# Mixer A of a two-block network on one core: two heads stacked on the rows, directions as planes of one tile, level products over 64 rows

## The chip, the core and the metric

The kernel runs on one core of one Trainium2 chip. The metric is the device time of one execution in microseconds (us), from the first to the last instruction and what the runtime adds around them. A core has five instruction streams: TensorE (PE, whose weight loads are shown apart as PEld), VectorE (DVE), ScalarE (ACT), GpSimd (POOL) and SyncE (SP, which here only issues DMAs). Each stream runs in its own order and waits on semaphores of the others.

## The reference

The network has two layers of a first block and then one second block, on 512 latent tokens and 256 context tokens of width 1024, all in float32. A layer of the first block projects the tokens, runs four mixers A to D on 256 features each, gates their outputs, projects them back and normalises. Only mixer A is touched by the change. It is a gated linear recurrence with four heads of 64 features, run forwards and backwards, with forget gates f of their own for either direction:

```python
def gla_chunk_scan(q, k, v, logf, s0):
    """S_t = diag(f_t) S_{t-1} + k_t^T v_t ; o_t = q_t S_t"""
...
o_f, _ = gla_chunk_scan(q, k_f, i, lf_f, s_cf)
o_b, _ = gla_chunk_scan(flip(q), flip(k_b), flip(i), flip(lf_b), s_cb)
y = merge_heads(rms_norm(o_f + flip(o_b), norm_g))
```

Here k = 1 - f for each direction, q is silu of a projection, and i is the value. The latent scans start from the final state of the context (in layer 0 the context's outputs are wanted too, so 768 queries; in layer 1 only the 512 latent ones).

## The kernel before

Tokens are cut into chunks of 128 (six of them, four latent and two of the context). Within a chunk the products q_t k_s times the gates between s and t are found by doubling: `level_mm` is called once for the diagonal and once for each of seven levels i, with h = 2^i. At level i a block of 2h tokens meets: in the forward direction the queries of the upper half see the keys of the lower half, in the backward direction the queries of the lower half see the keys of the upper one. A mask `m8` picks from the 128 x 128 products those that belong to the level (`copy_predicated` into `att`). After the products of a level, q and k are multiplied by the gates of half a block (`T` holds these gates, multiplied together pair by pair), ready for the next level.

Before the change the 128 rows (partitions) of a tile hold one head: rows 0 to 63 its forward direction, rows 64 to 127 its backward one. `co_head` does one head, and `j_a` spawns it for both heads of a pair, so that two such generators go on side by side; pairs follow one another. At each level `co_head` makes `Qm`, a copy of `Qh` in which the queries that the level doesn't want are zeroed (mask `mq`); the matmul of a chunk then contracts over all 128 rows, both directions at once:

```python
self.mul("*", Qm.rearrange("p (c t) -> p c t", t=128), Qh.rearrange("p (c t) -> p c t", t=128), mq)
...
nc.tensor.matmul(ps[:, cc], Kh[:, cc], Qm[:, cc], start=True, stop=True)
```

Then four multiplications of 64 rows each bring `Qh` and `Kh` to the next level, and one brings `T` there. Two DMAs for each head copy the queries `qs` into the two halves of `Qm`. At the end of a head the keys are transposed, their products with the values `va` give the state's increments (`up`), and a chain of multiply-adds gives the state `Si` before each chunk. When both heads are done, `j_a` multiplies `att` by the values and `Si` by `Qh`, into a bank that `headnorm` reads.

The order of the work is not written by hand. The program keeps generators in flight (attention units, mixer A, normalisations) and a list of fillers (the projections, whose weights come by DMA and are split into two fp32r parts `whi` and `wlo`); while instructions are emitted, class `Est` estimates when each engine and each piece of data will be ready, and `turn` emits what could start first on PE, a filler if nothing else can. `best` chooses between DVE, POOL and ACT for an operation marked "*" by the same estimates. Each engine then runs its own stream in that order. A filler's products are three matmuls of fp32r; mixer A's are plain float32, which the trace shows as two records for each matmul. Every operation goes through one helper, so all rows of the profile carry the line L283; the names tell them apart. `banks` is PSUM, `kh`, `qh`, `qm`, `att`, `si`, `T`, `f` are the tiles named above (`si` is the state), `p` the probabilities of the attention mixers, `h` the projected tokens.

Of the kernel before, what the change touches and what calls it, by code (L numbers as in the profile page):

```python
# [13 lines left out]
AF = mybir.ActivationFunctionType  # L14
# [10 lines left out]
# column starts in w_in of the first block  # L25
# [25 lines left out]
# broadcast rows  # L51
# [37 lines left out]
def pack(inp):  # L89
# [40 lines left out]
    put("lb", g["hg_lb_logits"].reshape(2, 2, 4, 64).transpose(1, 3, 0, 2))  # L130
# [26 lines left out]
    # constants of the shapes  # L157
# [6 lines left out]
    mq = [np.where(p < 64, (t >> i) & 1, 1 - ((t >> i) & 1)) for i in range(7)]  # L164
    ms = [((p >> (i + 1)) == (t >> (i + 1))) & ((p >> i) != (t >> i)) for i in range(7)]
    a["masks"] = np.stack(mq + ms, axis=1).astype(f)
# [5 lines left out]
    # second block  # L172
# [32 lines left out]
class Quiet:  # L205
    """Stands for an engine while lifetimes are recorded."""
# [5 lines left out]
class Est:  # L212
    """Estimates, while instructions are emitted, of when engines and data will be ready: the order of emission follows."""
# [7 lines left out]
    def touch(self, ap):  # L221
        """The times of a tensor and the granules of it (128 elements) that ap covers."""
# [44 lines left out]
class Eng:  # L267
    """An engine whose instructions are timed as they are emitted."""
# [37 lines left out]
class Act:  # L306
    """Work in flight: a generator that yields what it waits for."""
# [6 lines left out]
class Tl:  # L314
    """A piece of SBUF with its own tensor."""
# [14 lines left out]
class Mem:  # L330
    """SBUF by lifetimes. A first emission (plan None) only records them; place() then gives each piece its address."""
# [82 lines left out]
class Pb:  # L414
    """Banks of PSUM."""
# [9 lines left out]
class Psum:  # L425
# [3 lines left out]
    def pick(self, n, est):  # L429
        """The free banks that have been read first, and when."""  # L430
# [28 lines left out]
class K:  # L459
# [18 lines left out]
    # ---- short forms  # L478
# [48 lines left out]
    def scale(self, out, a, s):  # L527
        """out = a times a column s."""
# [21 lines left out]
    # ---- time  # L550
    def time(self, eng, op, outs, ins, kw):
# [11 lines left out]
        if eng == "P":  # L563
            if op == "transpose":
                c = 107.0
            else:
# [27 lines left out]
    # ---- work in flight  # L594
# [11 lines left out]
    def after(self, *keys):  # L606
        """Until no work of these keys is in flight."""
# [70 lines left out]
    def choose(self):  # L678
        """Takes up the first filler for which there is room."""
# [37 lines left out]
    # ---- weights  # L717
# [28 lines left out]
    def more(self):  # L746
        """Weights of a further filler."""
# [17 lines left out]
    def g_fm(self, parts, evac):  # L765
        """parts: [(hi, lo, n)]; evac(i, bank) for each."""
# [1749 lines left out]
```

## Time and profile before

| | |
|---|---|
| median of 3 runs | 2021.99 us (2017.59, 2021.99, 2022.09) |
| span of the profiled execution | 2020.4 us, 1.6 us below the median; its time with what lies around the span is not given apart |
| instructions | 28590 |
| mixer A, layer 0 | about 191 to 476 us: the first pair of heads to 325 us, the second from 359 us |
| mixer A, layer 1 | about 814 to 1016 us |
| second block | from about 1150 us to the end, not touched |

Busy times are unions of the records of a group; the length of a matmul record includes its way through the array, so consecutive ones overlap, and what one costs is read from start to start. An idle engine costs nothing unless the end waits for it; here the stream to watch is PE's.

### The profile page before, as it was taken

Reading aid. Unit: us, or ns where it says so; the run is one execution under the profiler, and the core shown is the slowest. Engines: PE = TensorE matmul, PEld = TensorE weight load, DVE = VectorE, ACT = ScalarE, POOL = GpSimd, SP = SyncE. Lnnn points to the kernel's source line nnn. Section 1 sums busy time; section 2 is a strip of 40 time slices with the busy share of each in tenths; the row PEclk is TensorE's granted clock in tenths of the full one; section 3 lists DMA queues with packets and bytes.
Section 4 is the critical chain, followed back from the end, with each engine's and each line's share of the span. In section 5 each row is a group of like instructions: output and inputs, shape, how many; then the busy total and the mean of one; then the engine's idle time right before and its main releaser. Section 6 shows DMA issues by size and latency. Waiting matters only on the chain.

```text
span 2020.4 us, 28590 instructions
## 1 busy us (share of the span) xinstructions
PE 1892.4 (94%) x11270; PEld 1571.6 (78%) x11270; DVE 1295.5 (64%) x2202; ACT 621.0 (31%) x1274; POOL 636.4 (31%) x583
## 2 busy tenths in 40 slices
PE   6899889889999999979899989899999999999999
PEld 4688657789877788867787777877878787888887
DVE  2558885686557738787967878874533566545542
ACT  2245434414540135544335231143432211100100
POOL 1314662374232414565633353421121220000000
PEclk9999999999999999999999998999999999999999
DMA  8112241001132401103124221111232222233122
GB/s 348 53 32 71 72 142 47 17 17 57 32 115 84 157 1 43 38 21 106 43 63 141 98 101 66 67 58 48 81 128 87 99 73 84 83 115 115 53 84 73
DMA packets 46807, 162.32 MB, mean 80 GB/s; under 512 B 5312, under 2 KB 5824, under 8 KB 46416
## 3 DMA queue, kind: packets, MB, share of 16 engines
q1 hardware_dynamic: 43648, 151.63, 21.9%
q10 hardware_dynamic: 3024, 8.85, 1.3%
q8 instruction: 89, 1.46, 0.3%
q14 instruction: 46, 0.38, 0.1%
HBM read 152.58 MB, written 5.26 MB: 78 GB/s over the span
## 4 chain that ended last, share of the span: by engine, by line
PE 41%; DVE 11%; POOL 3%; issue 2%; ACT 2%; DMA 0%; ACTq 0%; DVEq 0%; POOLq 0%
PE banks L283 41%; DVE cacc L283 2%; POOL t L283 1%; DVE sm L283 1%; DVE wlo L283 1%; DVE kh L283 1%; DVE t L283 1%; ACT p L283 1%; DVE att L283 1%; DVE p L283 1%; DVE h L283 1%; DVE whi L283 0%; POOL h L283 0%; DMA ld<-gws 0%; DVE gt L283 0%
## 5 line engine op out<-in xcount | busy, mean ns | idle before, releaser
L283 PE MATMUL banks<-h,whi 128*128 128x512 f32 (+1 forms) x1968 | 583.9, 380 | 4.4 <-ACT h L283 2.1
L283 PEld LDWEIGHTS banks<-h,whi 128*128 128x128 f32 x1968 | 353.6, 191 | 66.5 <-POOL h L283 2.5
L283 PE MATMUL banks<-h,wlo 128*128 128x512 f32 (+1 forms) x984 | 369.4, 376 | 0.3 <-DVE wlo L283 0.3
L283 PE MATMUL banks<-whi,h 128*128 128x256 f32 (+3 forms) x1344 | 336.1, 333 | 17.2 <-DVE h L283 7.9
L283 DVE TENSOR_TENSOR wlo<-raw,whi 128x1024 fp32r<-128x1024 f32 (+1 forms) x174 | 216.6, 1248 | 94.9 <-PE banks L283 59.5
L283 PEld LDWEIGHTS banks<-whi,h 128*128 128x128 f32 x1344 | 235.5, 193 | 41.9 <-DVE h L283 9.8
L283 POOL TENSOR_TENSOR wlo<-raw,whi 128x1024 fp32r<-128x1024 f32 (+2 forms) x42 | 103.4, 2464 | 482.8 <-PE banks L283 314.6
L283 PE MATMUL banks<-wlo,h 128*128 128x256 f32 (+3 forms) x672 | 220.2, 328 | 7.4 <-POOL wlo L283 3.7
L283 PEld LDWEIGHTS banks<-h,wlo 128*128 128x128 f32 x984 | 187.6, 191 | 35.8 <-DVE wlo L283 1.0
L283 ACT ACTIVATE p<-banks,sm 128x768 f32<-128x768 f32 (+5 forms) x192 | 141.3, 739 | 107.5 <-DVE sm L283 90.6
L283 DVE TENSOR_REDUCE sm<-banks 128x1 f32<-128x768 f32 (+5 forms) x192 | 139.9, 750 | 49.1 <-PE banks L283 41.4
L283 PE MATMUL banks<-whi,hid 128*128 128x512 f32 x512 | 159.5, 392 | 0.0
L283 DVE CAST whi<-raw 128x1024 fp32r<-128x1024 f32 (+2 forms) x105 | 79.3, 759 | 112.8 <-DMA raw<-wm 66.0
L283 PEld LDWEIGHTS banks<-wlo,h 128*128 128x128 f32 x672 | 129.7, 193 | 19.0 <-DVE wlo L283 5.0
L283 ACT CAST whi<-raw 128x1024 fp32r<-128x1024 f32 (+2 forms) x83 | 82.8, 1002 | 193.3 <-PE banks L283 98.1
L283 PEld LDWEIGHTS banks<-whi,hid 128*128 128x128 f32 x512 | 96.1, 188 | 21.5
L283 PE MATMUL banks<-ident,p 128*128 128x128 f32 x656 | 97.1, 278 | 15.7 <-ACT p L283 5.7
L283 ACT COPY p<-banks 128x768 f32<-128x768 f32 (+5 forms) x122 | 75.6, 626 | 106.5 <-PE banks L283 96.8
L283 PE MATMUL banks<-qm,kh 128*128 128x128 f32 x640 | 91.9, 294 | 17.3 <-DVE att L283 8.1
L283 PEld LDWEIGHTS banks<-qm,kh 128*128 128x128 f32 x640 | 83.1, 204 | 29.4 <-issue 9.8
L283 PEld LDWEIGHTS banks<-ident,p 128*128 128x128 f32 x656 | 74.5, 141 | 34.3 <-ACT p L283 8.7
L283 POOL TENSOR_TENSOR t<-t,mhalf 128x1 f32<-128x1 f32 (+5 forms) x51 | 64.4, 1266 | 115.9 <-DVE t L283 112.3
(331 smaller groups left out, 3220.8 us busy)
## 6 DMA issues: line engine op xcount, KB each, us to landing
raw<-wm SPq DMA_DIRECT2D x64, 512.0 KB, 3.7
raw<-win SPq DMA_DIRECT2D x60, 512.0 KB, 3.6
raw<-wada SPq DMA_DIRECT2D x48, 512.0 KB, 4.8
raw<-wgate SPq DMA_DIRECT2D x32, 512.0 KB, 3.2
raw<-wout SPq DMA_DIRECT2D x24, 512.0 KB, 3.5
raw<-w2f SPq DMA_DIRECT2D x10, 512.0 KB, 3.2
xr<-xtok SPq DMA_DIRECT2D x6, 512.0 KB
x<-z SPq DMA_DIRECT2D x6, 512.0 KB, 2.6
```

The costliest lines, as they stand in the source:

```text
L283: return f(*a, **kw)
```

## The change

Everything that mixer A does between the projections and its head norm is laid out anew. Rows 0 to 63 hold head 0 of the pair and rows 64 to 127 head 1; the two directions are planes of one tile ([128, 2, 768]). The units of `w_in` and the columns of the lower bounds are packed to fit. `j_a` does a whole pair in one generator (`co_head` is gone). At a level it copies the keys that the level wants, forward ones for lower halves and backward ones for upper halves, into `ks`; the wanted queries are read in place by a view that steps between the planes (`aview`). A chunk's products are then two matmuls of 64 rows, one for each head in turn, into two banks. `Qm`, its mask `mq`, the load of `mq` and the 16 DMAs of the queries are gone. The multiplications to the next level are one for q and one for k, over 128 rows. The products with the values have 64 instead of 128 stationary columns, the state is brought on by half as many instructions of 128 rows, and the last products add two of 64 rows for each head and chunk where one of 128 rows stood. The outputs are copied out in pieces of 64 rows, and the squares are taken from the copy. The estimate takes half the time for a matmul of 64 rows.

```diff
-        for h in range(4):
-            u.append(_fm_unit(np.concatenate([w[:, C_FF + 64 * h:C_FF + 64 * h + 64], w[:, C_FB + 64 * h:C_FB + 64 * h + 64]], 1)))
+        for j in range(2):
+            u += [_fm_unit(w[:, c + 128 * j:c + 128 * j + 128]) for c in (C_FF, C_FB)]
...
+                    if k.shape[0] == 64:
+                        c /= 2
...
-    def level_mm(self, Kh, Qm, att, i):
+    def aview(self, z, flip, h, o, n):
+        N = z.f.shape[2]
+        p, at = z.f.ap[0], z.f.offset + o + (N if flip else 0)
+        return bass.AP(z.f.tensor, at, [list(p), [2 * h, n // (2 * h)], [h - N if flip else N + h, 2], [1, h]])
...
+    def aparts(self):
+        return ((0, 4), (4, 2))[:1 + self.full]
...
+    def half(self, v, j):
+        return bass.AP(v.tensor, v.offset + 64 * j * v.ap[0][0], [[v.ap[0][0], 64]] + [list(x) for x in v.ap[1:]])
...
+    def level_mm(self, lhs, rhs, att, i, c0, n):
...
-        for c in range(nch):
-            cc = slice(c * 128, (c + 1) * 128)
-            nc.tensor.matmul(ps[:, cc], Kh[:, cc], Qm[:, cc], start=True, stop=True)
-        n = nch * 128
+        ps = self.new_bank(2)
+        for c in range(n):
+            k, q = lhs(c0 + c), rhs(c0 + c)
+            for j in range(2):
+                nc.tensor.matmul(ps[:, j * 512 + c * 128:j * 512 + (c + 1) * 128], self.half(k, j), self.half(q, j), start=True, stop=True)
...
         for i in range(7):
-            yield (Qh,)
-            mq = self.mq[:, i, :].unsqueeze(1).to_broadcast([128, nch, 128])
-            self.mul("*", Qm.rearrange("p (c t) -> p c t", t=128), Qh.rearrange("p (c t) -> p c t", t=128), mq)
-            yield (Qm, Kh, self.bank(nb))
-            self.level_mm(Kh, Qm, att, i)
             h = 1 << i
...
+            yield (KZ,)
+            ks = M.new([128, nq], tag="ks")
+            self.cp("*", ks.rearrange("p (b w h) -> p b w h", w=2, h=h), self.aview(KZ, False, h, 0, nq))
+            for c0, n in self.aparts():
+                yield (QZ, ks, self.bank(2))
+                self.level_mm(at(ks), lambda c: self.aview(QZ, True, h, c * 128, 128), att, i, c0, n)
...
-            for r0, up in ((0, 1), (64, 0)):
-                r = slice(r0, r0 + 64)
-                tq = Tv[r, :nbq, 1 - up].unsqueeze(2).to_broadcast([64, nbq, h])
-                tk = Tv[r, :, up].unsqueeze(2).to_broadcast([64, nbk, h])
-                self.mul("*", Qv[r, :, up], Qv[r, :, up], tq)
-                self.mul("*", Kv[r, :, 1 - up], Kv[r, :, 1 - up], tk)
...
+            for z, flip, n in ((QZ, True, nq), (KZ, False, NT)):
+                v = self.aview(z, flip, h, 0, n)
+                self.mul("*", v, v, self.tview(Tc, flip, o, n // (2 * h), h))
...
+                for j in range(2):
+                    hh, r = 2 * pair + j, slice(64 * j, 64 * j + 64)
+                    cc = slice(c * 128, (c + 1) * 128)
+                    out = ps[r, j * 512 + (c - c0) * 128:j * 512 + (c - c0 + 1) * 128]
+                    nc.tensor.matmul(out, self.va[:, c, hh * 64:hh * 64 + 64], att[:, j, cc], start=True, stop=False)
+                    for d in range(2):
+                        nc.tensor.matmul(out, S[r, d, c], QZ[r, d, cc], start=False, stop=d == 1)
```

PE's stream in layer 0, second pair, early levels, before the change (out<-moving,stationary; numbers are buffers; `qm_3158` and `qm_3166` belong to the two heads, the other rows are attention scores, transposes and a projection):

```order
L283 MATMUL banks<-qm_3158,kh_3161 128x128 x6
L283 MATMUL banks<-ident_70,stg_3322 128x128 x2
L283 MATMUL banks<-whi_2976,h_98 128x256
L283 MATMUL banks<-wlo_2977,h_98 128x256
L283 MATMUL banks<-whi_2976,h_99 128x256
...
L283 MATMUL banks<-qm_3166,kh_3169 128x128 x6
L283 MATMUL banks<-whi_2976,h_99 128x256
L283 MATMUL banks<-whi_2976,h_98 128x256
L283 MATMUL banks<-wlo_2977,h_98 128x256
L283 MATMUL banks<-whi_2976,h_99 128x256
L283 MATMUL banks<-qm_3158,kh_3161 128x128 x5
```

The same place after the change (`ks_2963` and `ks_3078` are the key copies of two successive levels; `p` rows are outputs of mixer B):

```order
L282 MATMUL banks<-qh_2840,ks_2963 128x128 x12
L282 MATMUL banks<-p_2871,bdv_720 64x128
L282 MATMUL banks<-p_2880,bdv_720 64x128
...
L282 MATMUL banks<-whi_3054,h_98 128x256
L282 MATMUL banks<-whi_3054,h_97 128x256
L282 MATMUL banks<-wlo_3055,h_97 128x256
L282 MATMUL banks<-whi_3054,h_98 128x256
L282 MATMUL banks<-qh_2840,ks_3078 128x128 x12
```

Two groups of six for a level, one for each head and some work apart, have become one group of twelve; between these two levels stand 44 other matmuls.

POOL's stream in the same place, before (`qm` rows make the masked queries, `qh` and `kh` rows bring queries and keys to the next level; x2 are two equal rows):

```order
L283 TENSOR_TENSOR qh_3162<-qh_3162,T_3164 64x192x2
L283 TENSOR_TENSOR kh_3161<-kh_3161,T_3164 64x192x2 x2
L283 TENSOR_TENSOR qh_3162<-qh_3162,T_3164 64x96x4
L283 TENSOR_TENSOR kh_3169<-kh_3169,f_2961 64x384
L283 TENSOR_TENSOR qm_3166<-qh_3170,mq_67 128x768
L283 TENSOR_TENSOR qh_3170<-qh_3170,T_3172 64x192x2 x2
```

And after:

```order
L282 TENSOR_TENSOR qh_2840<-qh_2840,T_2841 128x192x2x2
L282 TENSOR_TENSOR wlo_3055<-raw_2967,whi_3054 128x1024
L282 TENSOR_TENSOR kh_2839<-kh_2839,T_2841 128x96x2x4
L282 TENSOR_SCALAR p_3044<-p_3044,sm_3043 128x256
L282 TENSOR_TENSOR qh_2840<-qh_2840,T_2841 128x96x2x4
```

The masked copies are gone, and one multiplication of 128 rows stands for four of 64. Over the whole program all 28 multiplications of q to a next level stand on POOL afterwards, 23 of the 28 of k on DVE; DVE has 2055 instead of 2204 instructions, POOL 458 instead of 588, PE 10002 instead of 9914.

PE's stream at the last products of the second pair of layer 0, before (`att` and `si` rows of the two heads):

```order
L283 MATMUL banks<-att_3163,va_531 64x128
L283 MATMUL banks<-qh_3162,si_3773 64x128
L283 MATMUL banks<-att_3171,va_531 64x128
L283 MATMUL banks<-att_3163,va_531 64x128
L283 MATMUL banks<-qh_3162,si_3773 64x128
L283 MATMUL banks<-att_3171,va_531 64x128
L283 MATMUL banks<-qh_3170,si_3890 64x128
```

And after:

```order
L282 MATMUL banks<-att_2842,va_529 64x128
L282 MATMUL banks<-qh_2840,si_3446 64x128 x2
L282 MATMUL banks<-att_2842,va_529 64x128
L282 MATMUL banks<-qh_2840,si_3446 64x128 x2
L282 MATMUL banks<-att_2842,va_529 64x128
```

Three matmuls a head and chunk instead of two, the last two of them over 64 rows. Counted over the whole stream, the part of the array that a matmul uses (its rows and columns) changes from one matmul to the next 264 times before and 379 times after.

## Rows read from the trace of the kernel before

**Rows 1.** The page, busy us (share of the span) and instructions

```profile
PE 1892.4 (94%) x11270; PEld 1571.6 (78%) x11270; DVE 1295.5 (64%) x2202; ACT 621.0 (31%) x1274; POOL 636.4 (31%) x583
```

**Rows 2.** Busy time by stage: stage; length, PE, PEld, DVE, ACT, POOL; clock, DMA

```profile
100.00:191.00 91.00, 86.90 (x650) 77.47 (x649) 62.27 (x120) 43.41 (x96) 25.44 (x21) 1.00 0.08 24
191.00:320.00 129.00, 115.72 (x799) 82.33 (x799) 103.82 (x178) 57.17 (x124) 79.88 (x75) 0.99 0.36 117
320.00:450.00 130.00, 116.16 (x918) 104.16 (x919) 93.77 (x152) 47.70 (x98) 57.81 (x56) 0.93 0.07 19
450.00:600.00 150.00, 146.39 (x1128) 130.02 (x1127) 88.20 (x217) 68.40 (x167) 54.79 (x50) 1.00 0.21 68
...
800.00:920.00 120.00, 102.30 (x720) 88.81 (x718) 99.47 (x145) 52.09 (x94) 70.34 (x77) 0.96 0.11 34
920.00:1020.00 100.00, 94.66 (x781) 78.67 (x781) 82.11 (x144) 42.69 (x78) 60.49 (x70) 0.98 0.23 72
1020.00:1150.00 130.00, 126.60 (x788) 103.72 (x789) 94.96 (x172) 48.42 (x105) 42.26 (x35) 1.00 0.28 93
```

**Rows 3.** Waits of PE over the whole span: us, times, longest

```profile
PE banks L283 <- DVE att L283: 11.8, 9, 3.1
...
PE banks L283 <- POOL qm L283: 4.1, 2, 2.9
```

**Rows 4.** PE by form: records | busy us, mean ns | idle before

```profile
L283 PE MATMUL banks<-qm,kh 128*128 128x128 f32 x640 | 91.9, 294 | 17.3 <-DVE att L283 8.1 <-POOL qm L283 4.1 <-DVE qm L283 2.0
```

**Rows 5.** PE in order of time: start, length, records [wait before]

```profile
440.94 1.57 PE L283 MATMUL banks<-qm,kh 128*128 128x128 f32 x12
442.26 0.37 PE L283 MATMUL banks<-whi,h 128*128 128x256 f32 x1
...
447.76 2.90 PE L283 MATMUL banks<-qm,kh 128*128 128x128 f32 x12 [3.14 <-DVE att L283]
450.31 0.56 PE L283 MATMUL banks<-whi,h 128*128 128x256 f32 x1
```

**Rows 6.** PE in order of time, layer 1, outputs of mixer C

```profile
868.81 1.53 PE L283 MATMUL banks<-p,vc 128*64 128x128 f32 x24
870.27 0.62 PE L283 MATMUL banks<-kc,qs 128*128 128x512 f32 x2
```

**Rows 7.** PE in order of time, products with two moving columns

```profile
320.67 1.50 PE L283 MATMUL banks<-cst,hq 128*128 128x2 f32 x12
322.04 0.94 PE L283 MATMUL banks<-kb,qs 128*128 128x512 f32 x4
```

**Rows 8.** PE in order of time, last products of a pair

```profile
1014.48 0.32 PE L283 MATMUL banks<-qh,si 128*64 128x128 f32 x1
1014.49 0.32 PE L283 MATMUL banks<-att,va 128*64 128x128 f32 x1
...
1016.16 0.39 PE L283 MATMUL banks<-whi,h 128*128 128x256 f32 x1
```

**Rows 9.** PE in order of time, entry into a block of 64-column products

```profile
337.86 0.62 PE L283 MATMUL banks<-h,whi 128*128 128x512 f32 x2
338.32 0.40 PE L283 MATMUL banks<-h,wlo 128*128 128x512 f32 x1
338.65 1.52 PE L283 MATMUL banks<-p,bdv 128*64 128x128 f32 x22
```

**Rows 10.** DVE by form, the products of mixer A

```profile
L283 DVE TENSOR_TENSOR kh<-kh,T 64x384 f32<-64x384 f32 x47 | 42.1, 896 | 0.8
...
L283 DVE TENSOR_TENSOR qm<-qh,mq 128x768 f32<-128x768 f32 x18 | 21.9, 1219 | 0.2
```

**Rows 11.** POOL by form, the products of mixer A

```profile
L283 POOL TENSOR_TENSOR kh<-kh,T 64x384 f32<-64x384 f32 x49 | 51.9, 1059 | 23.9 <-PE banks L283 22.0
...
L283 POOL TENSOR_TENSOR qm<-qh,mq 128x768 f32<-128x768 f32 x10 | 19.9, 1986 | 7.9 <-PE banks L283 7.5
```

More of the change, by code (lines that the diff above doesn't have):

```diff
@@ L163, in pack @@
     p, t = np.arange(128)[:, None], np.arange(128)[None, :]
-    mq = [np.where(p < 64, (t >> i) & 1, 1 - ((t >> i) & 1)) for i in range(7)]
     ms = [((p >> (i + 1)) == (t >> (i + 1))) & ((p >> i) != (t >> i)) for i in range(7)]
-    a["masks"] = np.stack(mq + ms, axis=1).astype(f)
+    a["masks"] = np.stack(ms, axis=1).astype(f)
     sel = np.zeros((128, 4), f)
@@ L1473, in level_mm, with j_a @@
         self.P.free(ps)
[L1475 removed]
+    def j_a(self, pair):
         nc, M, P = self.nc, self.M, self.P
         nq = self.nq
[L1479 to L1538 removed]
@@ L1540, in j_a @@
-    def j_a(self, pair):
-        nc, M = self.nc, self.M
-        nch = self.nq // 128
-        qs, fs = self.fq.pop(pair)
-        res = {}
-        for hh in range(2):
-            self.spawn("head", self.co_head(pair, hh, qs, fs[hh], res), 1)
-        yield (self.until(lambda: len(res) == 2),)
-        M.free(qs)
-        yield (self.bank(2 if self.full else 1),)
-        pvb, pv = self.pvs_new()
-        for c in range(nch):
-            for hh in range(2):
-                Qh, att, Si = res[hh]
-                h = 2 * pair + hh
-                cc = slice(c * 128, (c + 1) * 128)
-                o = pv(c)[hh * 64:hh * 64 + 64]
-                nc.tensor.matmul(o, self.va[:, c, h * 64:h * 64 + 64], att[:, cc], start=True, stop=False)
-                nc.tensor.matmul(o, Si[:, c, :], Qh[:, cc], start=False, stop=True)
-        for hh in range(2):
-            M.free(*res[hh])
-        self.headnorm(pvb, self.V(f"hg{self.l}"), pair, 4e-6)
+        qs, F = self.fq.pop(pair)
@@ new lines, in j_a @@
+        KZ, QZ, TZ = M.new([128, 2, NT], tag="kh"), M.new([128, 2, nq], tag="qh"), M.new([128, 2, NT], tag="T")
+        att, ks = M.new([128, 2, nq], tag="att"), M.new([128, nq], tag="ks")
+        for d in range(2):
+            self.ts("*", KZ[:, d], F[:, d], -1.0, 1.0, ALU.mult, ALU.add)
+            self.mul("*", QZ[:, d], qs.f, F[:, d, :nq])
+        self.add("*", ks.f, KZ[:, 0, :nq], KZ[:, 1, :nq])
+        at = lambda z: lambda c: z[:, c * 128:(c + 1) * 128]
+        for c0, n in self.aparts():
+            yield (ks, qs, self.bank(2))
+            self.level_mm(at(ks), at(qs), att, None, c0, n)
@@ new lines, in j_a @@
+        o = NT - 2 * (NT >> 7)
+        S = M.new([128, 2, 6, 64], tag="si")
+        for d in range(2):
+            yield (KZ, self.bank(2))
+            ps = self.new_bank(2)
+            for c in range(6):
+                nc.tensor.transpose(ps[:, c * 128:(c + 1) * 128], KZ[:, d, c * 128:(c + 1) * 128], self.ident.f)
+            self.cp("*", F[:, d], ps[:, :NT])
+            P.free(ps)
+        M.free(KZ)
+        for d, order in ((0, (4, 5, 0, 1, 2, 3)), (1, (5, 4, 3, 2, 1, 0))):
+            yield (F[:, d], self.bank())
+            up = self.new_bank()
+            for c in range(6):
+                for j in range(2):
+                    hh = 2 * pair + j
+                    nc.tensor.matmul(up[64 * j:64 * j + 64, c * 64:(c + 1) * 64], F[:, d, c * 128 + 64 * j:c * 128 + 64 * j + 64],
+                                     self.va[:, c, hh * 64:hh * 64 + 64], start=True, stop=True)
+            yield (up[:, 0:384],)
+            nc.gpsimd.memset(S[:, d, order[0]], 0.0)
+            for a, b in zip(order[:-1], order[1:]):
+                self.stt(S[:, d, b], S[:, d, a], TZ[:, d, o + a:o + a + 1], up[:, a * 64:(a + 1) * 64], ALU.mult, ALU.add)
+            P.free(up)
@@ new lines, in j_a @@
+        M.free(F, TZ)
+        y = M.new([128, nq], tag="hn")
+        for c0, n in self.aparts():
+            yield (S, QZ, att, self.bank(2))
+            ps = self.new_bank(2)
+            for c in range(c0, c0 + n):
+                for j in range(2):
+                    hh, r = 2 * pair + j, slice(64 * j, 64 * j + 64)
+                    cc = slice(c * 128, (c + 1) * 128)
+                    out = ps[r, j * 512 + (c - c0) * 128:j * 512 + (c - c0 + 1) * 128]
+                    nc.tensor.matmul(out, self.va[:, c, hh * 64:hh * 64 + 64], att[:, j, cc], start=True, stop=False)
+                    for d in range(2):
+                        nc.tensor.matmul(out, S[r, d, c], QZ[r, d, cc], start=False, stop=d == 1)
+            for j in range(2):
+                r = slice(64 * j, 64 * j + 64)
+                self.cp("*", y[r, c0 * 128:(c0 + n) * 128], ps[r, j * 512:j * 512 + n * 128])
+            P.free(ps)
@@ L1562, in j_a @@
+        M.free(S, QZ, att)
         if pair == 1:
             M.free(self.va)
+        yield (y,)
+        q = M.new([128, nq], tag="hq")
+        self.act(q.f, y.f, AF.Square)
+        self.spawn("hn", self.co_headnorm(y, q, self.V(f"hg{self.l}"), pair, 4e-6), 0)
     def co_transpose_h(self, xh, hh, o, mulv, addv):
@@ L2348, in g_block2 @@
         self.Y2, self.acc, self.tb = {}, {}, []
-        M.free(self.rope, self.mq, self.m8, self.cs, self.lbt)
+        M.free(self.rope, self.m8, self.cs, self.lbt)
         self.hbg = M.new([128, 32], F32, "hbg")
@@ L2390, in chain_a @@
         for pair in range(2):
-            yield (self.filled(f"fq{pair}{self.l}", f"v{self.l}"), self.room(24 * self.nq + 12 * NT), self.after("late"))
+            yield (self.filled(f"fq{pair}{self.l}", f"v{self.l}"), self.room(20 * self.nq + 16 * NT), self.after("late"))
             yield from self.j_a(pair)
```

86 lines of the change are left out of this document (24 added, 62 removed).

## The prediction

> **What bounds the kernel now.** I read the page's busy times first, then the stages, then PE's waits, then PE in order of time around the instructions that the change touches, and last the forms on DVE and POOL. PE is busy for 94% of the span, no other engine for more than 64% [rows 1]: the end moves when PE's own work or its idle time moves, and hardly otherwise. The stages show where PE is not full [rows 2]. In the four stages with mixer A (191 to 450 and 800 to 1020 us, 479 us together) it is idle for 13.3 + 13.8 + 17.7 + 5.3 = 50.2 us; in the three neighbours (371 us) for 4.1 + 3.6 + 3.4 = 11.1, which is 3.0%. At that share the four would idle 14.4 us, so some 36 us of idle time belong to mixer A. The granted clock falls there too: 0.99, 0.93, 0.96 and 0.98 of full, and the shortfall times the length is 1.3 + 9.1 + 4.8 + 2.0 = 17 us. DVE is busy 379 of the 479 us (79%) and POOL 269 (56%). PE's waits name the path: DVE's `att` for 11.8 us, POOL's `qm` for 4.1 [rows 3]; and 17.3 us of idle time stand just before the level products, which themselves cover 92 us in 640 records [rows 4].
>
> **PE's own work.** *The level products.* There are eight steps (the diagonal and seven levels) for 24 heads' chunks in layer 0 and 16 in layer 1: 320 matmuls, two records each, which are the 640 of rows 4. After the change there are also 320, since a chunk's two heads took one matmul each and now take one each of 64 rows. What changes is what one costs. Before, twelve records start 1.32 us before the next instruction, 110 ns each [rows 5]; I take 113, nearer the 114 of another group of the same stationary size [rows 7]. The trace of before has no product of 64 rows with the heads in turn. The nearest row is one in which two heads alternate between the two halves of the array's columns: 24 records with the same 128 moving columns in 1.46 us, 61 ns each [rows 6]. The pieces run beside each other there, and halves of the rows may do the same. If they do, the term is 640 x (61 - 113) = -33 us. The bounds are nothing (no overlap) and -37 (55 ns, half of the 110). I take -33, since the alternation is the very pattern of that row, with rows in the place of columns. The moving operand is now read by a strided view; no row shows what that costs, and at most it eats this term.
>
> *The products with the values* go from 48 of 128 stationary columns to 96 of 64 (6 chunks, 4 heads, 2 layers): 96 records of 114 ns become 192 of 61, +1 us (if a piece saved nothing, +11).
>
> *The last products* grow from two to three matmuls for each of the 40 heads and chunks: 80 records more. In the trace of before 26 records of this block take 1.68 us, 65 ns each [rows 8]: +5 us; at full 114 ns, +9.
>
> *Changes of the part of the array in use* rise from 264 to 379, by 115. One entry from full-width products into a block of 64 columns is in the trace [rows 9]: from its second row to the third, a single record, 0.33 us pass, where the two records ahead took 0.46, 0.23 each. I take 0.10 us a change: +11 us. The bounds are 0.03 (+4), if most are hidden, and 0.2 (+23), if both sides of a change pay. The Trainium skill, page "TensorEngine Tiling (Array Packing)", section "Key Properties", says that changing the tiling mode drains TensorE; the row's 0.1 us agrees, and by that rule each of the 115 costs something.
>
> So PE's work moves by -33 + 1 + 5 + 11 = -16 us.
>
> **The idle time.** DVE and POOL lose work. Layer 0's 28 masked copies of 768 columns (four heads, seven levels) cost 21.9 us on DVE and 19.9 on POOL [rows 10, 11]; they go, and layer 1's 28 of 512 columns with them. Half as many copies of `ks` of the same sizes come (one for a pair and level), spread over DVE, POOL and ACT. Four multiplications of 64 rows a head and level become two of 128 rows a pair. POOL took 1059 ns for 64x384 and 1986 for 128x768 [rows 11], so its time goes with columns, not rows: eight of 1.06 us become two of 1.99. The two rows of `kh` alone carry 94 us in 96 instructions [rows 10, 11]; the pattern halves that and as much for `qh`. Neither engine bounds the span, so this counts through PE's idle time only. Its cover: if DVE and POOL were as long as before, nothing would be gained here. I take half of the 36 us, -18, since the waits on `qm` vanish as such, those on `att` have an engine with less queued ahead of it, but a level still has to pass through the engines between two groups of products. Bounds 0 and -36. Of the 17 us of clock I give back a quarter, -4 (0 to -17), since the low stretches follow waits: at 447.76, after a wait of 3.14 us, the same twelve records take 2.55 us instead of 1.32 [rows 5], 212 ns each, which is the 1.2 GHz level instead of 2.4.
>
> The DMAs of the queries and the load of `mq` leave SP's queue. What else is queued there comes earlier, if at all; the waits that [rows 3] show are on engines, not on loads, so I cost it at nothing. The copies of the outputs in pieces of 64 rows double a few instructions on engines with slack; nothing as well, for the same reason.
>
> The sum is -16 - 18 - 4 = -38 us against the span of 2020.4, 1982; with the 1.6 us to the median, **1984 us**.
>
> **Rivals.** *The load of the stationary operand sets the pace.* Twelve records with only 2 moving columns take 1.37 us, 114 ns each [rows 7], as long as those with 128 moving columns: with 128 stationary columns the load alone can explain the 110. The 61 ns of rows 6 had 64 stationary columns, so they are explained by a shorter load as well as by columns side by side. The new level products still load 128 columns, over 64 rows. If two halves of the rows can't load at once, the first term is zero: 0 + 1 + 5 + 11 - 22 = -5, and a little more idle time can hide, so -5 to -9: some 2015 us on the median's scale. Against it: the two heads' loads go to different rows, as those of rows 6 go to different columns. No row decides between the two. The Trainium skill, page "TensorE: Matmul & The Clock Gate", section "LDWEIGHTS (loading the stationary operand)", says that the load's time goes with the stationary columns and not with the rows; by that the level records stay where they are and this rival holds. The Trainium skill's page "TensorEngine Tiling (Array Packing)", section "Key Properties", says that different tiles load and multiply in parallel; by that the first case holds.
>
> *One chain in place of two, slower.* Before, two heads' generators gave PE alternate groups of six matmuls with other work between; now one generator gives a group of twelve, and the next group can't start until its q product is through. That product reads and writes the tile in place, so it starts after the group's end, and all 28 stand on POOL at 1.99 us each, behind whatever POOL is doing, another 1 to 2 us. A gap that isn't filled costs as the one at 447.76 did: 3.14 us of waiting and 1.23 at the low clock, 4.4 us. If ten of the 28 levels pay that, +44 us; with the -16 of PE's work and nothing of the old idle time won, 2020.4 + 28 = 2048, 2050 as a median. It decides from four such waits on, more than what the -16 pay for (16 / 4.4). Against it: four pairs share 479 us, some 120 a pair, 15 for each of eight steps, and the step itself needs about 5.5 (1.5 for the group, 2 of waiting on POOL, 2 for the product); at the place shown in the order 44 other matmuls stand between two levels, which at 0.11 us or more are 4.8 us of cover. But at one other place PE's order leaves two matmuls only, so a few such waits will come.
>
> **How the numbers follow.** The first case has a chance of 0.60, with 1950 to 2008 as its own range: at the low end both idle time and clock come back nearly whole, at the high end the changes of tiles cost 0.2 us each and nothing of the idle time is won. The load as the pace has 0.24, 2015 give or take 10; one chain as the bound 0.16, from 2022 upwards. What a measurement of this kernel can tell from no change is about 0.3%, 6 us. Faster by more than that (below 2016): 0.58 of the first case and 0.12 of the second, 0.70. Within it: 0.02, 0.10 and 0.02, 0.14. Slower: 0.02 of the second and 0.14 of the third, 0.16. The range for 8 in 10 is 1950 to 2026: it leaves out most of the third case and the best of the first.
>
> **What the profile of the changed kernel would show.** Twelve matmuls of `ks` (24 records) from their start to the next instruction in 1.5 us, the two heads' records starting together, if the first term holds; in 2.6 to 2.7 us if the load sets the pace. PE's busy time down by 10 to 20 us. Idle time of PE in the stages of mixer A near 32 us instead of 50, the granted clock there at 0.97 or more; if one chain is the bound, waits on POOL's `qh` of 2 to 4 us at several levels and a clock below 0.93. At an entry into a block of 64 rows, 0.1 us over the plain spacing; 0.2 and more would make the forecast too low by 10 us. DVE's and POOL's busy times down by some 50 to 100 us each. The forecast is wrong if the strided view slows the moving operand, and if fillers, placed anew by the estimate, leave idle time outside mixer A.

## The result and the profile after

The changed kernel takes 1986.86 us (median of four runs, 1982.71 to 1992.85) where the kernel before takes 2022.04 beside it: a ratio of 0.983, 95% interval 0.981 to 0.985, 35 us less. The forecast was 1984 (1950 to 2026). The profiled execution spans 1987.1 us.

The page's busy times, which answer to [rows 1]:

```profile
PE 1871.8 (94%) x11446; PEld 1542.3 (78%) x11446; DVE 1199.5 (60%) x2053; ACT 623.6 (31%) x1277; POOL 527.4 (27%) x453
```

PE is still the engine that sets the end, at the same share of a shorter span. DVE lost 96 us and POOL 109. The stages, with the columns of [rows 2] (the products of mixer A now run from 225 to 435 and from 821 to 968 us, where they ran from 221 to 476 and from 843 to 1016, so the same stretch holds more of the other work than before):

```profile
100.00:191.00 91.00, 85.54 (x642) 76.16 (x641) 60.69 (x116) 42.11 (x92) 26.62 (x23) 1.00 0.06 19
191.00:320.00 129.00, 122.28 (x915) 89.86 (x915) 87.88 (x155) 58.08 (x123) 40.50 (x37) 0.92 0.25 86
320.00:450.00 130.00, 123.41 (x1080) 101.52 (x1078) 74.86 (x137) 51.82 (x102) 52.96 (x47) 0.97 0.15 50
450.00:600.00 150.00, 144.13 (x1027) 122.93 (x1024) 86.76 (x203) 69.69 (x174) 37.25 (x34) 1.00 0.19 65
800.00:920.00 120.00, 106.99 (x834) 86.87 (x833) 80.39 (x120) 53.19 (x92) 57.75 (x50) 0.96 0.10 32
920.00:1020.00 100.00, 96.82 (x819) 78.67 (x818) 61.12 (x103) 39.01 (x74) 29.51 (x37) 1.00 0.23 75
1020.00:1150.00 130.00, 118.89 (x711) 96.71 (x710) 101.53 (x177) 55.35 (x116) 46.59 (x37) 0.99 0.33 109
```

In the four stages of mixer A PE is idle for 6.7 + 6.6 + 13.0 + 3.2 = 29.5 us, where it was 50.2; DVE is busy for 304 us of the 479 instead of 379, POOL for 181 instead of 269. The granted clock has not come back there: its shortfall is 10.3 + 3.9 + 4.8 + 0 = 19 us, against 17. Two of the neighbours got emptier: 450 to 600 us idles 5.9 (3.6 before) and 1020 to 1150 us 11.1 (3.4). Over the whole span PE's idle time fell by 12.7 us, from 128.0 to 115.3 (the span less PE's busy time).

The groups of PE that the change touches (records; busy time, mean length; idle time before them), answering to [rows 4]:

```profile
L282 PE MATMUL banks<-qh,ks 64*128 64x128 f32 x560 | 48.5, 309 | 9.2 <-POOL qh L282 5.3 <-DVE sm L282 1.2 <-ACT ks L282 1.0
...
L282 PE MATMUL banks<-qh,si 64*64 64x128 f32 x160 | 25.7, 283 | 0.0
...
L282 PE MATMUL banks<-att,va 128*64 128x128 f32 x80 | 17.3, 298 | 0.0
...
L282 PE MATMUL banks<-qs,ks 64*128 64x128 f32 x80 | 7.3, 316 | 3.8 <-POOL ks L282 3.8
L282 PE MATMUL banks<-va,f 128*64 128x64 f32 x192 | 7.2, 225 | 0.0
```

and what PE waited for among mixer A's tiles (us, times, longest), answering to [rows 3]:

```profile
PE banks L282 <- DVE att L282: 8.0, 8, 2.4
...
PE banks L282 <- POOL qh L282: 5.3, 3, 3.4
PE banks L282 <- POOL ks L282: 4.4, 3, 2.6
```

`qm` is gone from this list, `att` went from 11.8 to 8.0 us, and in its stead come 5.3 us on POOL's `qh` and 4.4 on `ks`: a handful of waits, the longest 3.4 us, not one at every level. Just before the level products PE now idles 9.2 + 3.8 = 13.0 us, where it was 17.3 [rows 4].

Two groups of level products in order of time, one of 16 records in layer 1 and one of 24 in layer 0, each with the row behind it:

```profile
854.70 1.16 PE L282 MATMUL banks<-qh,ks 64*128 64x128 f32 x16
855.79 0.73 PE L282 MATMUL banks<-h,whi 128*128 128x512 f32 x2
```

```profile
393.60 1.61 PE L282 MATMUL banks<-qh,ks 64*128 64x128 f32 x24
395.14 0.66 PE L282 MATMUL banks<-p,bdv 128*64 128x128 f32 x8
```

From start to the next instruction's start these take 1.09 and 1.54 us. Eight more records cost 0.45 us, 56 ns each, and what is left over is 0.2 us: the change of shape on the way in and the one on the way out, about 0.1 each. In the single records of the first group two start 5 to 7 ns apart each time, and the next two 112 ns later (0.21 us after the first two); the weight loads go in the same pairs, 182 to 188 ns long. So two halves of the rows load and multiply at once.

The diagonal's products, whose moving operand is read without the strided view, take the same time, 1.09 us from start to start:

```profile
899.48 1.16 PE L282 MATMUL banks<-qs,ks 64*128 64x128 f32 x16
900.57 0.44 PE L282 MATMUL banks<-ident,stg 128*128 128x128 f32 x2
```

The last products do not look like that:

```profile
298.87 0.43 PE L282 MATMUL banks<-att,va 128*64 128x128 f32 x2
299.23 0.65 PE L282 MATMUL banks<-qh,si 64*64 64x128 f32 x4
299.81 0.43 PE L282 MATMUL banks<-att,va 128*64 128x128 f32 x2
```

A head and chunk takes 0.94 us (298.87 to 299.81), six records, one after the other: within a shape they start 109 ns apart (160 ns from the first to the second), and from one shape to the next about 200 ns pass. In the kernel before, 26 records took 1.68 us [rows 8], so a head and chunk (four records) took 0.26.

When all records of PE in each execution are taken from start to the next start, less the waits that the profile names, the difference of the two spans splits up as follows (us; the forecast's 11 us of shape changes are split by where the trace has them: 52 more at the level groups, 73 more at the last products, five fewer elsewhere):

```
                          before    after   difference   forecast
level products, 640 rec.    81.6     52.9      -28.7     -33 + 5
products with the values    10.6      6.5       -4.1     +1
last products               11.3     37.3      +26.0     +5 + 7
all other records         1789.9   1775.9      -14.0  \
named waits                114.4    101.9      -12.5  /  -18 - 4
sum                                            -33.3     about -38
```

A wait counts as named only from the modelled end of the record ahead of it, so short ones lie in the line above; those two lines belong together. The sum leaves out the time ahead of PE's first record and behind the start of its last.

### The profile page after: what moved, and what is told of

Read it like the earlier page. It is cut to its first block, busy times and chain, and to the rows that moved or that the text cites. A ratio compares the mean times of both kernels' runs of the same rounds, so it can differ in the third digit from the quotient of the medians.

```text
span 1987.1 us, 28567 instructions
## 1 busy us (share of the span) xinstructions
PE 1871.8 (94%) x11446; PEld 1542.3 (78%) x11446; DVE 1199.5 (60%) x2053; ACT 623.6 (31%) x1277; POOL 527.4 (27%) x453
## 4 chain that ended last, share of the span: by engine, by line
PE 40%; DVE 13%; issue 4%; POOL 4%; ACT 1%; DMA 1%; ACTq 0%; POOLq 0%; DVEq 0%; SPq 0%
PE banks L282 40%; DVE cacc L282 3%; POOL t L282 2%; DVE t L282 1%; DVE wlo L282 1%; DVE sm L282 1%; DVE z L282 1%; DVE p L282 1%; DVE h L282 1%; ACT p L282 1%; DVE whi L282 0%; DVE gt L282 0%; DVE xr L282 0%; POOL p L282 0%; POOL qh L282 0%
## 5 line engine op out<-in xcount | busy, mean ns | idle before, releaser
L282 DVE TENSOR_TENSOR wlo<-raw,whi 128x1024 fp32r<-128x1024 f32 (+2 forms) x175 | 222.6, 1275 | 106.2 <-PE banks L282 59.7
L282 ACT CAST whi<-raw 128x1024 fp32r<-128x1024 f32 (+2 forms) x88 | 88.3, 1007 | 223.3 <-PE banks L282 147.4
L282 DVE CAST whi<-raw 128x1024 fp32r<-128x1024 f32 (+2 forms) x103 | 73.2, 715 | 116.0 <-PE banks L282 98.0
L282 PE MATMUL banks<-wlo,hid 128*128 128x512 f32 x256 | 99.6, 389 | 0.0
L282 ACT ACTIVATE rl<-banks 128x512 f32<-128x512 f32 (+1 forms) x35 | 19.7, 562 | 169.2 <-PE banks L282 169.2
```

Of the source, the lines that this page charges most:

```text
L282: return f(*a, **kw)
```

## The experiments

Each run's ratio is to the kernel before on the same chip; "x us from the changed kernel" is the difference of the two ratios times 2021 us.

**The heads not in turn.** The same level products, head by head within a bank; the order on every engine is otherwise the changed kernel's.

```diff
-        for c in range(n):
-            k, q = lhs(c0 + c), rhs(c0 + c)
-            for j in range(2):
+        for j in range(2):
+            for c in range(n):
+                k, q = lhs(c0 + c), rhs(c0 + c)
```

> The level products of a bank are written out head by head instead of in turn; nothing else moves on any engine. If the two halves of the rows run beside each other only because they alternate (the theory), a record goes back from 56 ns to 107 to 115 ns: 640 x 55 = +35 us, some 2020 us, and no faster than the kernel before. If a product of 64 rows is shorter by itself (the rival), a record stays near 56 ns and the time within 5 us of the changed kernel.

1996.89 us, ratio 0.9885 (0.9858 to 0.9911): 12 us slower than the changed kernel, a third of what the theory expected and more than the rival did. The same group of layer 1 in order of time:

```profile
854.43 1.71 PE L282 MATMUL banks<-qh,ks 64*128 64x128 f32 x16
856.07 0.50 PE L282 MATMUL banks<-h,whi 128*128 128x256 f32 x2
```

1.64 us instead of 1.09, 90 ns a record when the two changes are taken off, where no overlap would give 111. The single records show why. They do not name the head, but they fall into two series: one starts at 854.43 and goes on, after a first step of 0.21 us, at 112 ns up to 855.32; the other starts at 854.99, when the first still has three to come. That record at 854.99 is 0.37 us long, as the one at 854.43 is and as both heads' first ones are in the changed kernel; all others here are 0.27. I read it as the second head's first, so products of the other half of the rows were taken up ahead of ones that stand before them in the stream. In the groups of eight (four records a head) nearly everything overlaps even so: 0.65 us against 0.64 in the group that starts at 283.12 here and at 278.25 in the changed kernel. Over the kernel the level products take 72.1 us instead of 52.9, 19 more, and named waits fell by 8 against it. So a product of 64 rows is not shorter by itself (one head alone goes on at 112 ns), which settles the rival; writing the heads in turn is worth some 12 us here, and the rest of the overlap comes without it.

**The last products regrouped.** All products of `att` first, then the states' with the heads in turn. All chunks of a head now stand in one group in its bank: `start` is set on the first product of the group alone, and `stop` on the last.

```diff
             for c in range(c0, c0 + n):
                 for j in range(2):
...
-                    nc.tensor.matmul(out, self.va[:, c, hh * 64:hh * 64 + 64], att[:, j, cc], start=True, stop=False)
-                    for d in range(2):
-                        nc.tensor.matmul(out, S[r, d, c], QZ[r, d, cc], start=False, stop=d == 1)
...
+                    nc.tensor.matmul(o_(c, j), self.va[:, c, hh * 64:hh * 64 + 64], att[:, j, cc], start=c == c0, stop=False)
+            for c in range(c0, c0 + n):
+                for d in range(2):
+                    for j in range(2):
...
+                        nc.tensor.matmul(o_(c, j), S[r, d, c], QZ[r, d, cc], start=False, stop=d == 1 and c == c0 + n - 1)
```

> The last products are regrouped: all products of att with the values first, then all of the states with the heads in turn. In the changed kernel they take 37.3 us in 240 records, 26 more than before. If the changes of the tile's shape and the two heads' states standing behind each other cost that (the theory), 240 records go to about 60 ns, some 14 us, and the kernel to 1987 - 23 = 1964 us (1960 to 1972). If the wait for the head norm and the next stage takes most of it (the rival), 1980 us or more.

1966.18 us, ratio 0.9727 (0.9699 to 0.9754), 20 us faster than the changed kernel. The last products of a pair in order of time:

```profile
294.73 1.09 PE L282 MATMUL banks<-att,va 128*64 128x128 f32 x16
295.76 1.96 PE L282 MATMUL banks<-qh,si 64*64 64x128 f32 x32
297.65 0.66 PE L282 MATMUL banks<-att,va 128*64 128x128 f32 x8
298.24 1.09 PE L282 MATMUL banks<-qh,si 64*64 64x128 f32 x16
299.26 0.44 PE L282 MATMUL banks<-ident,p 128*128 128x128 f32 x2
```

All 72 records take 4.5 us where twelve heads' chunks took 0.94 each. Over the kernel it is 16.6 us instead of 37.3, and nearly all of that 20.7 us reached the end.

**Grouped within a chunk only.**

```diff
...
                 for j in range(2):
...
-                    nc.tensor.matmul(out, self.va[:, c, hh * 64:hh * 64 + 64], att[:, j, cc], start=True, stop=False)
-                    for d in range(2):
-                        nc.tensor.matmul(out, S[r, d, c], QZ[r, d, cc], start=False, stop=d == 1)
...
+                    nc.tensor.matmul(out[j], self.va[:, c, hh * 64:hh * 64 + 64], att[:, j, cc], start=True, stop=False)
+                for d in range(2):
+                    for j in range(2):
+                        nc.tensor.matmul(out[j], S[rr[j], d, c], QZ[rr[j], d, cc], start=False, stop=d == 1)
```

> The last products grouped only within a chunk: both heads' products of att first, then the four of the states with the heads in turn; 40 shape changes where the regrouped kernel has about 12 and the changed kernel 80. If a change costs about 0.1 to 0.15 us and two heads side by side save half of the rest (the theory), 240 records x 55 ns + 40 x 0.14 = 19 us instead of 37.3, 1968 to 1973 us. If the shape changes alone cost (heads in turn save nothing), 240 x 111 ns + 40 x 0.14 = 32 us, 1981 us. If the turn alone matters and changes are free, as the regrouped kernel: 14 to 16 us.

1968.52 us, ratio 0.973 (0.971 to 0.9751); the last products take 20.3 us:

```profile
295.83 0.44 PE L282 MATMUL banks<-att,va 128*64 128x128 f32 x4
296.20 0.66 PE L282 MATMUL banks<-qh,si 64*64 64x128 f32 x8
296.79 0.44 PE L282 MATMUL banks<-att,va 128*64 128x128 f32 x4
```

0.37 us for four records of `att` and 0.59 for eight of the states, 0.96 a chunk. Against the regrouped kernel the twelve records overlap in the same way, and there are 28 more changes for 3.7 us, 0.13 us each. At that price the 66 changes fewer of the regrouped kernel (10 within the block instead of 76) are worth some 9 of its 20.7 us; the other 12 come from having the two heads side by side.

**The estimate without its halving.** The two lines that halve the cost of a matmul of 64 rows are taken out.

> The estimate no longer takes half the time for a matmul of 64 rows; only the order of the work moves. If the layout makes the gain (the theory), within 10 us of the changed kernel either way. If the order that the halved estimate finds makes it (the rival), slower by 12 us or more.

1991.79 us, ratio 0.9852 (0.9827 to 0.9878): 5 us from the changed kernel, with overlapping intervals. The layout makes the gain.

**Load put back on DVE and POOL.** Two multiplications for each level of a pair, read by nobody.

```diff
+            for _ in range(2):
+                zz = M.new([128, nq], tag="zz")
+                iz = self.ident.f.unsqueeze(1).to_broadcast([128, nq // 128, 128])
+                self.mul("*", zz.rearrange("p (c t) -> p c t", t=128), iz, iz)
+                M.free(zz)
```

> Two products of constants of the size of the old masked copies are added for each level of a pair, put on DVE or POOL by the same rule and read by nobody; about 28 x 2 x 1.2 to 2 us = 70 to 100 us of engine time, what the change took off. If the idle time of PE in mixer A fell because these engines have less queued (the theory), PE's idle time there goes back up and the time rises by 10 to 20 us. If it fell because fewer groups wait (one chain, one product per step; the rival), by 4 us at most.

1994.61 us, ratio 0.9873 (0.9843 to 0.9904), 9 us slower. DVE got 36 us and POOL 44 more. The four stages of mixer A (length; PE, PEld, DVE, ACT, POOL; clock):

```profile
191.00:320.00 129.00, 115.54 (x863) 84.42 (x862) 92.86 (x154) 55.43 (x111) 54.72 (x44) 0.92 0.26 87
320.00:450.00 130.00, 117.91 (x1019) 97.34 (x1019) 88.78 (x148) 52.98 (x105) 58.64 (x47) 0.96 0.15 50
800.00:920.00 120.00, 106.51 (x850) 86.67 (x849) 91.57 (x137) 55.32 (x97) 66.59 (x55) 0.97 0.08 27
920.00:1020.00 100.00, 97.50 (x847) 80.24 (x846) 62.04 (x108) 42.22 (x77) 39.60 (x44) 1.00 0.25 80
```

PE idles 13.5 + 12.1 + 13.5 + 2.5 = 41.5 us there instead of 29.5. So 80 us of work on these engines came with 12 of the 21 us of idle time that the change had taken off; over the whole span it is 8.4 us more. The 9 us lie between the theory's 10 and the rival's 4, the two intervals still overlap a little, and other orders of the same work moved the time by as much ("Other orders", below): this run does not decide.

**The kernel before without its masked copies.** What `mq` takes out of the queries is left in.

```diff
-            self.mul("*", Qm.rearrange("p (c t) -> p c t", t=128), Qh.rearrange("p (c t) -> p c t", t=128), mq)
-            yield (Qm, Kh, self.bank(nb))
-            self.level_mm(Kh, Qm, att, i)
+            yield (Qh, Kh, self.bank(nb))
+            self.level_mm(Kh, Qh, att, i)
```

> The kernel before without the 56 masked copies of q: the levels' products take the unmasked q, so unwanted queries enter them (this part of the computation is left out). DVE and POOL lose some 70 us, and a level loses a step of 1.2 to 2 us ahead of its products. If PE's idle time in mixer A hangs on these engines (the theory: half of 36 us), faster than the kernel before by 8 to 20 us. If the overlapped level products are the whole gain (the rival), within 4 us.

2007.45 us, ratio 0.9923 (0.9901 to 0.9945): 16 us faster than the kernel before, with level products as slow as ever.

```profile
191.00:320.00 129.00, 115.92 (x831) 87.88 (x830) 97.31 (x181) 53.57 (x109) 58.62 (x61) 0.92 0.36 120
320.00:450.00 130.00, 125.89 (x1068) 112.59 (x1066) 80.99 (x191) 66.79 (x149) 26.15 (x33) 1.00 0.06 17
800.00:920.00 120.00, 107.15 (x819) 93.09 (x818) 97.14 (x163) 50.22 (x95) 73.47 (x91) 0.99 0.14 41
920.00:1020.00 100.00, 96.44 (x752) 78.27 (x751) 69.84 (x131) 35.09 (x63) 37.15 (x47) 1.00 0.24 75
```

```profile
450.00:600.00 150.00, 139.83 (x985) 121.65 (x983) 107.39 (x195) 52.75 (x119) 63.37 (x64) 0.98 0.20 66
```

```profile
PE 1883.2 (94%) x11270; PEld 1570.5 (78%) x11270; DVE 1278.5 (64%) x2208; ACT 612.3 (31%) x1250; POOL 563.4 (28%) x545
```

DVE lost 17 and POOL 73 us. In the four stages PE idles 13.1 + 4.1 + 12.8 + 3.6 = 33.6 us instead of 50.2, but they do not hold the same work: the products of layer 0's second pair now run from 491 to 563 us, in the stage 450 to 600, which idles 10.2 us instead of 3.6. Over the whole span PE's idle time fell by 4.3 us, from 128.0 to 2006.9 - 1883.2 = 123.7, and its busy time by 9.2. So the 16 us lie in the theory's range and away from the rival's 4, but they are not the idle time of these stages alone; and since a step of each level went together with the load, the run cannot tell the two apart.

**Other orders.** The constant of the estimate for the lag of a result is 95 instead of 90 ns, first in the kernel before.

> The kernel before with another constant in its estimate (the lag of a result, 95 instead of 90 ns), so the same work in another order. If the order alone moves the time little (the theory), within 8 us of the kernel before. If the gain of the change could be a better draw of the order (the rival), a time more than 15 us away from it.

2034.5 us, ratio 1.0054 (1.0029 to 1.0079): 11 us slower, between the two marks. Then in the changed kernel.

> The changed kernel with 95 instead of 90 ns in its estimate, so the same work in another order: the counterpart of the kernel before in another order, which was 11 us slower. If an order is worth some 10 us either way (the theory), between 1977 and 1999 us, still at least 15 us faster than the kernel before. If the changed kernel's order was a lucky one (the rival), 2005 us or more.

1990.89 us, ratio 0.9841 (0.9818 to 0.9864), 3 us from the changed kernel. The three runs that only changed the order moved the time by 11, 3 and 5 us (the last is the one without the halving); the gain of the change, 35 us, is not such a draw.

**The multiplications of q on DVE,** on top of the regrouped last products.

```diff
-                self.mul("*", v, v, self.tview(Tc, flip, o, n // (2 * h), h))
+                self.mul("v" if flip else "*", v, v, self.tview(Tc, flip, o, n // (2 * h), h))
```

> On top of the regrouped last products, all multiplications of q to the next level go to DVE instead of POOL. POOL takes 1.75 us (768 columns) and 1.26 us (512), DVE about 0.98 and 0.69: the way through a level gets shorter by 0.6 to 0.8 us, 28 times, but DVE gets 24 us more. If POOL's product is what PE waits for in the chain of levels (a rival of the prediction), the waits on it (5.3 us in the changed kernel) go and the time falls by 5 to 10 us from the regrouped kernel's. If it is mostly covered (the theory), within 4 us either way.

1962.84 us, ratio 0.9703 (0.9682 to 0.9723), 5 us under the regrouped kernel, with overlapping intervals. The multiplications on DVE (count; busy time, mean ns; the four of level 0, which read `f`, are left out), and then PE's waits on mixer A's tiles:

```profile
L282 DVE TENSOR_TENSOR qh<-qh,T 128x768 f32<-128x768 f32 x12 | 11.3, 940 | 0.0
...
L282 DVE TENSOR_TENSOR qh<-qh,T 128x512 f32<-128x512 f32 x12 | 8.7, 727 | 0.0
```

```profile
PE banks L282 <- POOL ks L282: 6.8, 3, 3.7
...
PE banks L282 <- DVE att L282: 2.5, 4, 1.1
...
PE banks L282 <- DVE qh L282: 0.7, 1, 0.7
```

The waits on POOL's `qh` are gone (0.7 us on DVE's instead), and those on `ks` rose from 4.1 in the regrouped kernel to 6.8. Whether DVE is the better place was put to the other order too.

> The kernel with regrouped last products and the multiplications of q on DVE, in the other order too (95 ns). If the 3 to 5 us by which DVE beat POOL there are the order's (the theory), this one is anywhere from 1955 to 1975 us. If DVE is really the better engine (the rival), at or below 1963 us, and below the regrouped kernel's 1966.

1970.54 us, ratio 0.9743 (0.9722 to 0.9765), above the regrouped kernel. So the 5 us are within what an order is worth, and the place of this multiplication is not shown to matter. The regrouped kernel with q on POOL was not run in the other order. The fastest version that was run is the regrouped kernel with q on DVE, at 1963 us; the regrouping alone carries all of its gain that is clear.

## Why the prediction was right, and where it was not

**The level products** were forecast at -33 us with 61 ns a record, less the changes at their edges. They run at 56 ns and cost -28.7 with the changes, against -28. The row with two halves of the columns [rows 6] was the right one to carry over to halves of the rows. The strided moving operand costs nothing that shows: the diagonal's groups, read without it, take the same 1.09 us. The rival that the load sets the pace was wrong in its conclusion. Each head's records do go at the pace of 128 stationary columns: 112 ns over 64 rows, and 112 ns over 128 rows with two moving columns (the single records of [rows 7]). The Trainium skill, page "TensorE: Matmul & The Clock Gate", section "LDWEIGHTS (loading the stationary operand)", says that the load's time goes with the columns and not with the rows, and the two 112 agree. But two loads run at once: the two heads' records start 5 to 7 ns apart. The Trainium skill, page "TensorEngine Tiling (Array Packing)", section "Key Properties", says that different tiles load and multiply in parallel, and the trace agrees. One ground of this rival could have been tested in the trace of before: it put the 61 ns of [rows 6] down to a shorter load as well as to pieces side by side, but the single records of that block start in pairs 6 to 7 ns apart and each half goes on at 109 ns, so being side by side explains all of it.

**The changes of shape** were priced at 0.10 us, which the level groups confirm (0.2 for a way in and out); between the two kinds of 64-column products it is 0.13 (the chunk-wise run). The changes came to 120 in the trace, five more than forecast.

**The last products** are the step that failed: "80 records more" at 65 ns, +5 us, and some 7 us for their share of the changes. They cost +26. The 65 ns came from a row in which the two heads' products overlapped; in the new order the `att` product and the states' of one head stand between those of the other, with a change of shape on either side, and the two or four records of one head and shape have nothing beside them. So not only the added records go at 110 ns, all 240 do: 240 x 0.11 = 26 us, and with 76 changes at 0.13 it is 36, near the 37.3. Even the forecast's upper bounds together (+9, and 0.2 us for each of 73 changes, 15) reach only 24. The regrouped and the chunk-wise run confirm this: with the heads in turn the same 240 records take 16.6 and 20.3 us.

**The products with the values** gained 4 us instead of losing 1: two heads of 64 columns stand side by side there, and 192 records take 34 ns each, not the 61 that were taken from a row with 128 moving columns.

**The idle time** was forecast at -18 with a guess of one half, and the clock at -4, in all -22. In mixer A's stages 21 us of idle time went and none of the clock came back (0.92 in the first of them, where the forecast's sign was 0.97 or more); over the whole span the mean granted clock is 0.979 before and 0.980 after. The named waits and the other records of the whole span together give -26.5. So the size was near, but why they fell is not shown. The runs can be set side by side by taking the level products, the products with the values and the last products off the span (us):

```
                                             rest of the span
the kernel before, in its two orders         1917, 1929
the kernel before without masked copies      1906
the changed layout, no load added, 8 kernels 1878 to 1898 (the changed kernel 1890)
the changed kernel with load put back        1897
```

Each figure is of one execution, and executions of one kernel differ by up to 10 us. That the new layout has less of this rest holds in every order that was run. The load put back stays inside what the other orders give, so it shows no cost of its own. The masked copies taken out give less than either order of the kernel before, so they are likely to be a part of it; whether by the engines' load or by the shorter way through a level stays open. Part of what mixer A gave up was given back later (the two stages named above idle 10 us more), as the forecast's last sentence feared. I take it that the other work drawn forward into mixer A is missing there as cover, but no run tests that.

**The chain of one generator per pair** did not decide, though two of its signs came in part: PE waits on POOL's `qh` and `ks` for 9.7 us in all, in six waits, and the clock of the first stage is 0.92, below the 0.93 named for it. But what PE idles just before the level products fell from 17.3 to 13.0 us, so there was mostly other work for PE between the levels; moving q's product to a faster engine changed nothing clear.

That 1984 came within 3 us owes something to errors of opposite sign (+14 at the last products, -5 at the values, -4 in idle time and the rest); and with other orders of the same work 3 to 11 us away, the same sum could have missed by that much.

## What to carry to other kernels

When two groups of matmuls can share the array, the price of a record hangs on who stands next to it in the stream as much as on its own shape (here 240 records took 37.3, 20.3 or 16.6 us by their order alone): cost every product of the new order by its neighbours, the ones that are merely rearranged too. Put products of one shape together and alternate the halves within them. Where PE idles between dependent steps, work taken off the engines in between may count even if none of them is ever the bound: 90 us of masked copies taken out gained 16 us here, more than any mere change of order moved, while 80 us put back cost 9, which such a change can do too. And where a program chooses its own order, run the same work in another order before a difference of this size is given a cause.

## What was not expected of the hardware

Products of one half of the rows were started ahead of products of the other half that stand before them in the program, as far as the length of the records tells the heads apart: with the heads not in turn, the second head's first record began three records (0.33 us) before the first head's last. So short runs of each head (four records) overlap almost wholly without any care for the order, and runs of eight by less than half.

In the products with the values, 64 stationary and 64 moving columns with two heads in turn cost 34 ns a record, against 110 for 128 stationary columns with 64 moving before the change:

```profile
291.98 0.92 PE L282 MATMUL banks<-va,f 128*64 128x64 f32 x24
292.73 0.28 PE L282 MATMUL banks<-p,vc 128*64 128x128 f32 x1
```

Both sides had to be short for that. In the single records each head goes on at 58 ns here, and two go side by side; where only the stationary side has 64 columns (the last products) a record follows its like after 109 ns, and where only the moving side has (the products with the values before) after 112.
